# Moving one pair of weight buffers 192 bytes up in SBUF, in a decoder block on one Trainium2 core

## The chip, the core and the metric

The kernel runs on one core of one Trainium2 chip. The metric is the device time of one execution in microseconds (us); the lower, the better. A kernel is timed in several runs, and the median stands for it. One further execution is profiled: its trace gives the start and the duration of each instruction, the waits and the transfers.

## The reference: what is computed

One decoder layer over 512 positions and 1024 channels, in float32. After a normalization, one wide projection feeds a gated short convolution and a sparse attention; both are merged through gates and an output projection and added to x. Then comes the feed-forward part, in which the change lies:

```
h = rmsnorm(x, norm2_g[l])
gu = h @ w_ffn_in[l]
g = causal_dwconv(gu[..., :D_FF], ffn_conv_w[l]) + ffn_conv_b[l]
x = x + (jax.nn.silu(g) * gu[..., D_FF:]) @ w_ffn_out[l]
```

D_FF is 2816, or 22 tiles of 128 channels; `w_ffn_in` has a gate half and an up half.

## The kernel before

**Precision.** All large products run as float32r, with each operand split into a high part and a low part. A product of weights W and activations X is then three matmuls: W high by X high, W high by X low, W low by X high. `dense` (lines 433 to 441) writes them down: for each weight tile first the two with the high weights (lines 437 and 438, alternating), and after all of these the ones with the low weights (line 440). Every matmul has a weight load of its own, of 128 columns (512 bytes in each partition), and TensorE loads the weights of the next matmul while the present one streams.

**The feed-forward input projection** (`ff_strassen`, `ff_forms`, `ff_pair`). Two tiles of 128 output channels are computed together, for the gate half (n = 0) and then for the up half (n = 1): 11 times 2, so 22 pairs. Each pair is one step of Strassen's scheme in Winograd's form: 7 products of quarter size instead of 8. A product has 4 tiles along the contraction and moves 256 positions, so it is 12 matmuls of 128x256, and a pair is 84. The activation forms lie in two long buffers, `xf_h` and `xf_l`, as 4 times 7 blocks of 256 floats. The weight forms of the seven products come from these buffers:

- a22 (one product): `th` (high, two buffers in turn) and `tl` (low), of 2048 bytes in each partition. `dma_split` fills them: ScalarE copies the raw weights into `th` (line 173), writes their negative into `tl` (line 174), and a DMA adds the weights again to `tl` (line 175).
- a11 and a12 (two products): `wh_s` and `wl_s`, from a ring that the down projection uses as well.
- the four sums of quarters: `sh` and `sl`, filled by `split` (lines 167 and 168).

**The down projection** (`down_part`) has matmuls of 128x512 with weights `wh_d` and `wl_d` from the same ring and activations `ah` and `al`; a part is two output tiles of 12 matmuls.

**Order of the work.** The scheduler orders each engine's instructions. In the long steady part of the feed-forward, from about 444 us of the span on, TensorE runs pair after pair as the code has it: the a22 product first (eight matmuls with `th`, four with `tl`), then the other six products (72 matmuls), then one part of the down projection (24 matmuls), then the next pair. Before that, between about 347 and 444 us, products of two pairs and parts of the down projection are interleaved.

**Where the buffers lie.** A partition of SBUF is one range of addresses. The pools `px` and `pw` lie behind one another and are filled in the order of the first request for each name; that is what the two lines of the change set. These are the starts in each partition, in bytes, of the program before, and what is left when they are divided by 128:

| Buffer | Start | mod 128 |
|---|---|---|
| `xf_h`, `xf_l` (moving, pairs) | 37152, 65824 | 32, 32 |
| `th`, two buffers | 94496, 96544 | 32, 32 |
| `gap_w` (never read or written) | 98592 | - |
| `tl`, two buffers | 98784, 100832 | 96, 96 |
| `sh`, first; `sl`, first | 111072; 123360 | 96; 96 |
| ring `wh` (`wh_s`, `wh_d`), first; ring `wl`, first | 204768; 217056 | 96; 96 |
| `ah`, first; `al`, first (moving, down projection) | 138720; 153056 | 96; 96 |

All further buffers of a name, and all slices that a matmul reads of them, lie whole multiples of 512 bytes on, so that the last column holds for each matmul. In words: a matmul of a pair moves data that start at 32 modulo 128; its weights start at 96, other than those of `th`, which start at 32 as the moving data do. In the down projection both start at 96.

Of the kernel before, what the change touches and what calls it, by code (L numbers as in the profile page):

```python
# [11 lines left out]
F32 = mybir.dt.float32  # L12
# [6 lines left out]
P = 128  # L19
# [66 lines left out]
def tile_block(ctx: ExitStack, tc: tile.TileContext, xT, pos, par, par2, w_tok, w_a3, w_gate, w_ao, w_bo, w_o,  # L86
# [13 lines left out]
    def const(shape, name, dt=F32, pool=sb):  # L100
        return pool.tile(shape, dt, name=name, tag=name)
# [798 lines left out]
    xf_h = const([P, 4, 7, TH], "xf_h", F32R, px)  # L900
    xf_l = const([P, 4, 7, TH], "xf_l", F32R, px)
    pw = ctx.enter_context(tc.tile_pool(name="pw", bufs=1, side="left"))
    pw.tile([P, D // 2], F32R, name="th_", tag="th", bufs=2)
    const([P, 48], "gap_w", F32, pw)

    def x_forms(k, v):
        nc.vector.tensor_sub(v[:, T1:T3 + 1], v[:, 1:4:2], v[:, 0:2])
# [282 lines left out]
```

## Time and profile before

| | us |
|---|---|
| Median of 3 runs | 696.2 (695.93 to 697.58) |
| The profiled execution: its own time | 696.92 |
| its span, first to last instruction | 695.1 |
| TensorE busy (matmul) | 689.2 |
| TensorE busy (weight load) | 614.5 |
| VectorE busy | 511.7 |
| ScalarE busy | 436.7 |
| GpSimd busy | 248.7 |

How to read the profile's rows: PE is TensorE's matmuls, PEld its weight loads, DVE VectorE, ACT ScalarE, POOL GpSimd. Names stand for buffers, with their numbers left out: `p<-xf_h,th` is a matmul into a PSUM tile whose name begins with p, with xf_h as moving data and th as weights. A row of the table by stretches of time has the stretch, its length, then for each engine the busy time and in brackets the number of instructions, the granted clock of TensorE as a share (1.00 is full), and the DMA share and GB/s. That number counts the instructions that run at any moment of the stretch: as a matmul of a pair is shown with some 0.28 us and the next starts after about 0.115 us, it holds two or three that began before. Durations of matmuls overlap and their ends are modelled; what a matmul costs in a stream without gaps is the distance from its start to the start of the next, and this text calls that distance a **step**.

### The profile page before, as it was taken

The page shows a single profiled execution, that of the slowest core. Times are in us where ns is not written, and L with a number is a line of the kernel's source. Part 1 is how long each engine was busy: PE and PEld are TensorE (multiplying, and loading weights), DVE is VectorE, ACT ScalarE, POOL GpSimd, SP SyncE. Part 2 cuts the span into 40 slices and gives each one's busy share as a digit, 9 for nine tenths or more (in the row PEclk, how much of TensorE's full clock was granted, in tenths as well). Part 3 has the DMA queues.
Part 4 walks back from the last instruction along what each step waited for, and adds up shares of the span by engine and source line. Part 5 has one row for each costly group of instructions (what it writes and reads, how often), then busy time and mean ns, then how long its engine had stood idle before and what let it go on. Part 6 is the DMA issues. An engine that isn't in the chain of part 4 may idle for free.

```text
span 695.1 us, 11268 instructions
## 1 busy us (share of the span) xinstructions
PE 689.2 (99%) x4111; PEld 614.5 (88%) x4111; DVE 511.7 (74%) x897; ACT 436.7 (63%) x776; POOL 248.7 (36%) x247
## 2 busy tenths in 40 slices
PE   9999999999999999999999999999999999999997
PEld 9999888887878888788889999999999999999986
DVE  6987886766566546475888999898787787877543
ACT  7635654878888866535776857665566655566530
POOL 4041443477788867462112212121122211112110
PEclk9999999999999999999999999999999999999999
DMA  8333686568666654563586977997877979775665
GB/s 268 113 98 122 170 194 145 132 240 237 222 222 228 195 169 124 193 229 118 130 198 160 219 192 167 245 218 180 215 173 180 210 172 227 174 175 112 132 137 152
DMA packets 57623, 124.87 MB, mean 180 GB/s; under 512 B 5344, under 2 KB 21088, under 8 KB 57568
## 3 DMA queue, kind: packets, MB, share of 16 engines
q1 hardware_dynamic: 35648, 79.39, 35.3%
q0 software_dynamic: 14848, 32.51, 27.4%
q10 hardware_dynamic: 7072, 12.26, 5.5%
q8 instruction: 32, 0.52, 0.3%
q14 instruction: 23, 0.19, 0.1%
HBM read 111.55 MB, written 12.58 MB: 179 GB/s over the span
## 4 chain that ended last, share of the span: by engine, by line
PE 95%; ACT 2%; DMA 1%; POOL 1%; DVE 1%; issue 0%; SPq 0%; ACTq 0%; POOLq 0%
PE p L438 10%; PE p L437 10%; PE p L440 10%; PE pdn L438 6%; PE pdn L437 6%; PE pdn L440 6%; PE pg L437 4%; PE pg L438 4%; PE pg L440 3%; PE pa L438 3%; PE pa L437 3%; PE pa L440 3%; PE po L438 2%; PE po L440 2%; PE po L437 2%; PE pj_s L269 2%
## 5 line engine op out<-in xcount | busy, mean ns | idle before, releaser
L437 PE MATMUL p<-xf_h,sh 128*128 128x256 f32 x336 | 80.6, 277 | 0.0
L438 PE MATMUL p<-xf_l,sh 128*128 128x256 f32 x336 | 80.5, 276 | 0.0
L175 POOL DMA_DIRECT2D wl_s<-in_w_ff_dram x22 | 19.6, 891 | 156.1 <-ACT wl_s L174 154.8
L438 PE MATMUL pdn<-al,wh_d 128*128 128x512 f32 (+1 forms) x176 | 68.5, 389 | 0.0
L437 PE MATMUL pdn<-ah,wh_d 128*128 128x512 f32 (+1 forms) x176 | 68.3, 389 | 0.0
L438 PEld LDWEIGHTS p<-xf_l,sh 128*128 128x128 f32 x336 | 63.1, 188 | 0.0
L437 PEld LDWEIGHTS p<-xf_h,sh 128*128 128x128 f32 x336 | 63.1, 188 | 0.0
L167 ACT ACTIVATE sh<-s 128x1024 fp32r<-128x1024 f32 x44 | 46.3, 1055 | 25.3 <-PE p L438 22.4
L168 DVE TENSOR_TENSOR sl<-s,sh 128x1024 fp32r<-128x1024 f32 x44 | 53.5, 1218 | 8.7 <-ACT sh L167 8.6
L173 ACT ACTIVATE wh_s<-wr_s 128x1024 fp32r<-128x1024 f32 x22 | 23.3, 1060 | 56.9 <-PE pdn L438 54.3
L750 POOL TENSOR_TENSOR tn_e<-tn_e,ph 128x512 fp32r<-128x512 f32 x40 | 51.2, 1294 | 16.2 <-ACT ph L749 16.0
L440 PE MATMUL p<-xf_h,sl 128*128 128x256 f32 x336 | 52.2, 277 | 0.0
L175 POOL DMA_DIRECT2D wl_d<-in_w_dn_dram x22 | 26.7, 1212 | 71.3 <-ACT wl_d L174 71.3
L437 PE MATMUL pg<-xg_h,wh_g 128*128 128x512 f32 x128 | 50.1, 392 | 0.0
L438 PE MATMUL pg<-xg_l,wh_g 128*128 128x512 f32 x128 | 50.1, 391 | 0.0
L440 PE MATMUL pdn<-ah,wl_d 128*128 128x512 f32 (+1 forms) x176 | 47.5, 388 | 0.0
L440 PEld LDWEIGHTS p<-xf_h,sl 128*128 128x128 f32 x336 | 44.7, 188 | 0.2
L1109 DVE TENSOR_TENSOR x<-x,pdn 128x512 f32<-128x512 f32 x47 | 32.0, 682 | 15.9 <-PE pdn L440 15.3
L150 POOL TENSOR_TENSOR wl_g<-wr_g,wh_g 128x1024 fp32r<-128x1024 f32 x16 | 38.5, 2405 | 10.4 <-ACT wh_g L148 9.7
L438 PE MATMUL p<-xf_l,wh_s 128*128 128x256 f32 x168 | 40.6, 277 | 0.0
L437 PE MATMUL p<-xf_h,wh_s 128*128 128x256 f32 x168 | 40.5, 277 | 0.0
L175 POOL DMA_DIRECT2D tl<-in_w_ff_dram x22 | 19.7, 894 | 57.3 <-ACT tl L174 49.7
(367 smaller groups left out, 2117.5 us busy)
## 6 DMA issues: line engine op xcount, KB each, us to landing
wr_s<-in_w_ff_dram SPq DMA_DIRECT2D x44, 512.0 KB, 5.0
wl_s<-in_w_ff_dram POOLq DMA_DIRECT2D x22, 512.0 KB, 7.8
wr_d<-in_w_dn_dram ACTq DMA_DIRECT2D x22, 512.0 KB, 8.3
wl_d<-in_w_dn_dram POOLq DMA_DIRECT2D x22, 512.0 KB, 9.0
wr_g<-in_w_gate_dram SPq DMA_DIRECT2D x16, 512.0 KB, 4.0
wr_a<-in_w_a_dram SPq DMA_DIRECT2D x12, 512.0 KB, 3.7
tl<-in_w_ff_dram POOLq DMA_DIRECT2D x22, 256.0 KB, 7.6
td_e<-e SPq DMA_DIRECT2D x16, 256.0 KB, 4.4
```

The lines of the kernel that those rows point to most:

```text
L150: e.tensor_sub(lo[:, 0:n], raw[:, 0:n], hi[:, 0:n].bitcast(F32))
L167: hi = nc.scalar.activation(h, v, AF.Copy)
L168: nc.vector.tensor_sub(l, v, h.bitcast(F32))
L173: nc.scalar.activation(h, raw, AF.Copy)
L175: nc.gpsimd.dma_start(l if dst is None else dst, src, accum_op=ALU.add)
L269: nc.tensor.matmul(acc, xg_h[:, k, ts_], wh, start=k == 0, stop=False)
L437: ops.append(nc.tensor.matmul(acc, wh, xh, start=first and i == 0, stop=False))
L438: ops.append(nc.tensor.matmul(acc, wh, xl, start=False, stop=False))
L440: nc.tensor.matmul(acc, wl, xh, start=False, stop=last and i == len(units) - 1)
L750: nc.gpsimd.tensor_sub(pl, pt, ph.bitcast(F32))
L1109: nc.vector.tensor_add(xj, xj, acc)
```

## The change

In the pool `pw`, the request for the 192 bytes of `gap_w` is moved from behind the request for `th` to ahead of it. The two buffers of `th` so start at 94688 and 96736, which is 96 modulo 128, where they started at 32; the gap lies at 94496. `tl` and all other buffers stay where they were, and the pool has the same size. On each engine the same instructions stand in the same order as before.

```diff
     pw = ctx.enter_context(tc.tile_pool(name="pw", bufs=1, side="left"))
+    const([P, 48], "gap_w", F32, pw)
     pw.tile([P, D // 2], F32R, name="th_", tag="th", bufs=2)
-    const([P, 48], "gap_w", F32, pw)
```

## The prediction

> **What bounds the kernel now.** I read the page first, for the engine that is never idle, then the same by stretches for the part of the span that the change touches.
>
> ```profile
> span 695.1 us, 11268 instructions
> PE 689.2 (99%) x4111; PEld 614.5 (88%) x4111; DVE 511.7 (74%) x897; ACT 436.7 (63%) x776; POOL 248.7 (36%) x247
> 360.00:690.00 330.00, 330.00 (x2368) 309.09 (x2367) 261.40 (x364) 194.17 (x256) 63.10 (x65) 1.00 0.78 181
> ```
>
> TensorE is busy for all 330.00 us of the feed-forward part, at a granted clock of 1.00, and nobody else comes near (VectorE 261.40). So here the time is the number of matmuls times their step, and a nanosecond that is put on a step or taken from it is seen at the end. No transfer, wait or order of instructions changes: what is left is what an address does to the step of a matmul. About 0.3% (2.1 us) is what a measurement of this kernel can tell from no change.
>
> Next I looked for a trace of the address in the groups by line and shape, mean ns behind the busy time:
>
> ```profile
> L437 PE MATMUL p<-xf_h,sh 128*128 128x256 f32 x336 | 80.6, 277 | 0.0
> L438 PE MATMUL p<-xf_l,th 128*128 128x256 f32 x84 | 21.1, 282 | 0.0
> L437 PE MATMUL p<-xf_h,th 128*128 128x256 f32 x84 | 21.0, 281 | 0.0
> L440 PE MATMUL p<-xf_h,tl 128*128 128x256 f32 x84 | 13.1, 277 | 0.0
> ```
>
> Same shape, same moving data, and `th` alone is 4 to 5 ns longer; `th` is also the one weight buffer that starts at 32 modulo 128 as the moving data do (the table of starts). `tl`, written from the same raw weights and read with the same block of `xf_h`, has 277. That looks like a small cost that the change takes away. But a mean can hide two values, so the third view is TensorE alone by stretches, cut at the starts of products (columns: stretch, length, PE busy with its count, clock, DMA share, GB/s). The counts hold two matmuls that began before the stretch (in two rows three).
>
> ```profile
> 358.83:360.84 2.01, 2.01 (x19) 1.00 1.05 220
> 374.08:404.50 30.42, 30.42 (x269) 1.00 0.91 219
> 379.30:380.25 0.95, 0.95 (x10) 1.00 1.02 403
> 406.34:411.76 5.42, 5.42 (x48) 1.00 0.96 232
> 411.76:412.71 0.95, 0.95 (x11) 1.00 1.04 377
> 412.71:417.69 4.98, 4.98 (x46) 1.00 0.34 105
> 424.09:428.45 4.36, 4.36 (x39) 1.00 0.39 161
> 443.90:444.85 0.95, 0.95 (x10) 1.00 1.12 276
> 444.85:453.46 8.61, 8.61 (x78) 1.00 0.88 197
> 453.46:458.93 5.47, 5.47 (x27) 1.00 0.95 215
> 655.22:663.83 8.61, 8.61 (x78) 1.00 0.69 150
> 443.90:669.30 225.40, 225.40 (x1622) 1.00 0.79 180
> ```
>
> The rows at 379.30, 411.76 and 443.90 are runs of eight matmuls with `th`: 0.95 / 8 = 118.8 ns a step. All other rows but 453.46 and the last hold matmuls of pairs with `wh_s`, `wl_s`, `sh`, `sl` or `tl` (that at 374.08 has three `th` runs within it), all with weights at 96 and moving data at 32. And these go at two paces: 358.83 with 2.01 / 17 = 118.2 ns, 406.34 with 5.42 / 46 = 117.8 and 424.09 with 4.36 / 37 = 117.8; but 412.71 with 4.98 / 44 = 113.2, 444.85 with 8.61 / 76 = 113.3 and 655.22 with the same. The clock is 1.00 in all of them, and the DMA share goes with neither (0.39 and 0.96 at the long pace, 0.34 and 0.91 at the short one). I call them the long pace (117.8) and the short pace (113.3).
>
> What switches between them is seen in the timeline (start, duration), at the end of one down part and the start of another pair:
>
> ```profile
> 405.89 0.39 PE L437 MATMUL pdn<-ah,wh_d 128*128 128x512 f32 x1
> 406.11 0.39 PE L438 MATMUL pdn<-al,wh_d 128*128 128x512 f32 x1
> 406.34 0.40 PE L437 MATMUL p<-xf_h,wh_s 128*128 128x256 f32 x2
> ...
> 423.18 1.07 PE L440 MATMUL pdn<-ah,wl_d 128*128 128x512 f32 x4
> 424.09 0.52 PE L440 MATMUL p<-xf_h,tl 128*128 128x256 f32 x3
> ```
>
> Where matmuls of a pair directly follow the 512-wide ones of the down or output projection, and their own weights start at 96, they take the long pace and keep it: the stretches 406.34 and 424.09 begin so, and 358.83 likewise behind the output projection. In the first of them 46 matmuls with `wh_s`, `wl_s`, `sh` and `sl` change nothing about it. Then comes the run of eight with `th` at 411.76, and behind it stands 113.2 ns. In the steady part a down part always comes ahead of `th`, and the pace behind `th` is short each time, from 444.85 to 655.22. So `th` does two things: it pays 118.8 ns a step itself, and it leaves the stream at the short pace for the 76 matmuls that follow, until the next 512-wide part loses it.
>
> **The change part by part.** ScalarE's writes and the DMA are not touched: `th` alone moves, the DMA of line 175 goes to `tl`, and the copy into `th` is off the path, since TensorE waits for nothing in 330 us. What TensorE reads is the whole change.
>
> *The `th` run itself, in the steady part.* With weights at 96 behind a down part it is what `wh_s` at 406.34 and `tl` at 424.09 are: eight steps of 117.8, or 0.942 us where 0.95 stands now, a gain of 0.008 us a pair. If the stream stayed at the short pace it would be 0.906, a gain of 0.044: that is the other end of this term.
>
> *The 76 matmuls behind it.* No matmul with weights at 32 comes any more, so nothing in the rows above brings the stream back from the long pace. 76 x (117.8 - 113.3) = 76 x 4.54 = 0.345 us a pair. The other end is zero, if the pace comes back by itself at once; I take the full value because the rows of matmuls at 96 behind a 512-wide one stay long for as far as they reach (46 and 37 matmuls), with each kind of weight buffer in them. The down part's own 5.47 us stay: it is entered from the short pace now and from the long one then, and I price that at nothing (its 24 matmuls start and end at 96 and 96 in both).
>
> *How many pairs.* One period is 0.95 + 8.61 + 5.47 = 15.03 us, and 225.40 / 15.03 is 15 pairs. So 15 x (0.345 - 0.008) = +5.06 us.
>
> *The interleaved stretch ahead of it.* From 412.71 to 417.69 the 44 matmuls at 113.2 go long as well: 44 x 4.6 = +0.20. From 374.08 to 404.50 no 512-wide matmul intervenes, and I expect the short pace to stay as it is; the three `th` runs in it then go at the short pace too: 3 x (0.95 - 8 x 0.1134) = -0.13 us. The remaining `th` runs, at 411.76 and 420, lie at the long pace already, so nothing.
>
> *Sum.* 5.06 + 0.20 - 0.13 = +5.1 us. Against the profiled execution's own 696.92 that gives 702.0; it lies 0.7 above the median of 696.2, for which I forecast 701.3. No cover is needed: TensorE is the bound before and after, and the others only gain time.
>
> The rows speak against a rule of the Trainium skill here. The page "SBUF — State Buffer", section "Who interferes with whom", gives TensorE two independent read ports, for moving data and for weights, and says "PE and ACT never wait on anyone"; the page "TensorE: Matmul & The Clock Gate", section "Step-by-step: what each phase is for", adds that loading the next weights takes no read bandwidth from the running matmul. By these the sum would be zero. The trace does not agree: 118.8 ns against 113.3 for matmuls that differ in the start of their weights.
>
> **The rivals.**
>
> *The small gain (faster side).* If the long pace came from something else in the neighbourhood of those stretches, the 168 matmuls with `th` would fall to 113.3 and the rest would stay: 168 x (118.8 - 113.3) = 0.92 us less, 695.3. For it: it is the plain reading of 282 against 277, and 15 of the pairs have no long step outside their `th` run today. Against it: the stretch 406.34, which has no `th` in it or near ahead of it and is long from its first matmul to its last. The point from which it decides: the `th` run can win 0.044 us a pair, and a long step costs 0.0045, so with ten long steps left in a pair of 84 the gain is gone.
>
> *The pace returns within the pair.* The longest unbroken row at the long pace behind a 512-wide part is 46 matmuls, and a pair has 84. If it came back half-way, 5.1 would be about 2.5, and the time 698.7. Nothing in the trace shows such a return; but nothing shows 84 without one either.
>
> *The short pace is lost earlier.* Its first appearance, at 374.08, isn't owed to a run of `th`:
>
> ```profile
> 373.15 0.28 PE L437 MATMUL p<-xf_h,wh_s 128*128 128x256 f32 x1
> ...
> 373.74 0.40 PE L419 MATMUL pr_n<-dg_n,ones 128*128 128x512 f32 x1
> 373.97 0.28 PE L438 MATMUL p<-xf_l,wh_s 128*128 128x256 f32 x1
> 374.08 0.62 PE L440 MATMUL p<-xf_h,wl_s 128*128 128x256 f32 x4
> ```
>
> There a 512-wide matmul with the weights `ones` (which do not start at 96) brings it. If it came out otherwise with `th` moved, the stretch 374.08 to 404.50 would be long too: (30.42 - 2.86) / 113.4 ns are 243 steps, 243 x 4.4 = 1.1 us, and the 0.13 would not come back: 702.5.
>
> *The address doesn't matter at all*, and `th` is dearer because it comes first in its pair: 696.2. Against it: at 379.30 a `th` run stands in the middle of the short pace, with no 512-wide matmul ahead of it, and has 118.8 all the same.
>
> **How the numbers follow.** The forecast, +5.1, has 0.62; the loss from 374 on 0.12; a return within the pair 0.10; the small gain 0.13; no effect 0.03. Slower by over 0.3%, or by over 2.1 us, are the first two and nearly all of the third: 0.83. Within 0.3% are the small gain, no effect and what is left: 0.16. Faster by over 0.3%, 0.01: the whole price of `th` is below 1 us. The range has the first three cases, 0.84 of the chance, from 698.7 to 702.5 and 0.7 above that for the spread of the runs (the profiled execution lies so far from the median): 698.7 to 703.2.
>
> **What would show it right or wrong.** In the changed kernel's trace, by the same stretches of the steady part: a period of 15.37 us where 15.03 stands, the eight `th` matmuls at 117.8 ns a step and the 76 behind them at 117.8 (8.95 us). The means of the groups: `sh` and `wh_s` go up from 277 towards 280, `th` down from 282 towards 280, all alike. The stretch before 404.50 stays at 113.4. It is wrong if the 76 stand at 113.3 (then the small gain is the case, and `th` does not carry the pace), or if the matmuls behind a down part start at 118 and fall to 113 in the middle of a pair.

## The result and the profile after

The changed kernel takes 702.84 us (median of 4 runs, 702.24 to 703.52) beside 696.54 for the kernel before on the same chip (4 runs, 695.93 to 697.58). The ratio is 1.0089, with a 95% interval of 1.0075 to 1.0103: 6.3 us slower. The profiled execution took 703.28, with a span of 701.5 us against 695.1: 6.4 us that can be looked for in the trace.

The page of the kernel after: TensorE is busy 6.2 us longer (695.4 against 689.2) with the same 4111 matmuls, and stays at 99%.

```profile
span 701.5 us, 11268 instructions
PE 695.4 (99%) x4111; PEld 620.3 (88%) x4111; DVE 512.7 (73%) x897; ACT 436.7 (62%) x776; POOL 247.4 (35%) x247
```

Two groups of it, by line and shape (busy time, mean ns of one):

```profile
L437 PE MATMUL p<-xf_h,sh 128*128 128x256 f32 x336 | 82.9, 279 | 0.0
L438 PE MATMUL p<-xf_l,th 128*128 128x256 f32 x84 | 20.9, 280 | 0.0
```

`th` has come down from 282 to 280, and `sh`, which wasn't touched, has gone up from 277 to 279. The second outweighs the first, since there are many more of the others. By these means alone the loss would still look small; the steps show its size. TensorE by stretches, cut at the same instructions as before (stretch, length, busy time with its count, clock, DMA share, GB/s):

```profile
373.83:405.28 31.45, 31.45 (x269) 1.00 0.84 210
413.49:418.43 4.94, 4.94 (x44) 1.00 0.51 187
445.09:446.03 0.94, 0.94 (x9) 1.00 1.15 259
446.03:454.98 8.95, 8.95 (x78) 1.00 0.96 236
454.98:460.46 5.48, 5.48 (x26) 1.00 0.82 172
661.26:670.21 8.95, 8.95 (x78) 1.00 0.68 153
445.09:675.69 230.60, 230.60 (x1622) 1.00 0.78 177
```

The 76 matmuls behind `th` take 8.95 us in the first steady pair and in the last, where 8.61 stood: 117.8 ns a step for 113.3, at a clock of 1.00 both times. The steady part is 230.60 us for 225.40, so 5.20 of the 6.4 us lie there. The stretch before the down projection begins, 373.83 to 405.28, has 31.45 us for 30.42: another 1.03. The last 0.4 lie around 418: the 42 steps from 413.49 to 418.43 are at 117.6 ns (4.94 us; before, the same 42 had 4.76, from 412.71 to 417.47), which is 0.18; and the four steps behind them (two of the pair, two of the down part) have 0.90 us where 0.69 stood, which is 0.21. With the 0.25 us by which this execution was ahead at 373.83 (374.08 before), the steady part begins 1.19 later (445.09 for 443.90), and 1.19 + 5.20 = 6.39 is the whole difference.

The 0.21 has a look of its own. TensorE and ScalarE at that place in the kernel after (start, duration; in brackets the idle time and what ended it):

```profile
418.55 0.28 PE L438 MATMUL p<-xf_l,sh 128*128 128x256 f32 x1
418.77 0.72 PE L437 MATMUL pdn<-ah,wh_d 128*128 128x512 f32 x2
419.33 0.28 PE L437 MATMUL p<-xf_h,sh 128*128 128x256 f32 x1
```

```profile
416.10 0.63 ACT L173 ACTIVATE th<-wr_s 128x512 fp32r<-128x512 f32 x1 [3.82 <-DMA wr_s<-in_w_ff_dram]
418.11 1.14 ACT L167 ACTIVATE ah<-up 128x512 fp32r<-128x512 f32 x2
```

The matmuls that read `ah` start while ScalarE is still writing its two halves (418.11 to 419.25); ScalarE is late because the copy into `th` ahead of it waited for raw weights until 416.10. This is a small stall, at a place that comes back below. The raw weights don't land there at the same time in each execution: the copy into `th` at this place starts at 414.06 in the kernel before, and between 413.42 (experiment 4) and 416.10 (here) in the traces whose order of work is the same.

### The profile page after: what moved, and what is told of

It is laid out like the page before. It is cut to its first block, busy times and chain, and to the rows that moved or that the text cites. A ratio compares the mean times of both kernels' runs of the same rounds, so it can differ in the third digit from the quotient of the medians.

```text
span 701.5 us, 11268 instructions
## 1 busy us (share of the span) xinstructions
PE 695.4 (99%) x4111; PEld 620.3 (88%) x4111; DVE 512.7 (73%) x897; ACT 436.7 (62%) x776; POOL 247.4 (35%) x247
## 4 chain that ended last, share of the span: by engine, by line
PE 89%; DMA 3%; ACT 3%; POOL 2%; DVE 1%; issue 1%; SPq 0%; ACTq 0%; POOLq 0%; DVEq 0%
PE p L437 10%; PE p L440 10%; PE p L438 10%; PE pdn L437 6%; PE pdn L438 6%; PE pdn L440 6%; PE pg L438 3%; PE pg L437 3%; PE pg L440 3%; PE pa L438 3%; PE pa L437 3%; PE pa L440 3%; PE po L438 2%; PE po L437 2%; PE po L440 2%; PE pj_s L269 2%
## 5 line engine op out<-in xcount | busy, mean ns | idle before, releaser
L437 PE MATMUL p<-xf_h,sh 128*128 128x256 f32 x336 | 82.9, 279 | 0.0
L438 PE MATMUL p<-xf_l,sh 128*128 128x256 f32 x336 | 82.8, 279 | 0.0
```

Of the source, the lines that this page charges most:

```text
L437: ops.append(nc.tensor.matmul(acc, wh, xh, start=first and i == 0, stop=False))
L438: ops.append(nc.tensor.matmul(acc, wh, xl, start=False, stop=False))
```

## The experiments

The theory was that of the prediction: the run of eight `th` matmuls, whose weights start where the moving data start, brings the short pace, and everything else in a pair only keeps the pace that it finds. Against it stood two rivals: that the place of `th` in memory as such (its address, its neighbours) sets the pace, or the place of the a22 product in the order, first behind the down part. What "start where the moving data start" means was open too: the table speaks of 128 bytes, and the period could be another. So `th` was first moved by other distances.

All kernels compute the whole result. Their edits are told against the kernel before, unless another is named. Below, **distance** is the start of the weights less the start of the moving data, modulo 256 (why 256 is the outcome of the second and of the eleventh experiment). From the table of starts, the kernel before has 0 for `th`, 192 for all other weights of a pair, and 0 in the down part; the kernel after has 192 for `th`.

**1. `th` higher by 64 bytes instead of 192** (distance 64).

```diff
+    const([P, 16], "gap_v", F32, pw)
     pw.tile([P, D // 2], F32R, name="th_", tag="th", bufs=2)
-    const([P, 48], "gap_w", F32, pw)
+    const([P, 32], "gap_w", F32, pw)
```

> The two th buffers lie 64 bytes higher than before (192 in the change), so at 96 modulo 128 as in the change. Theory (what counts is whether weights and moving data start alike modulo 128; a run that starts alike leaves the short pace): the same as the change, eight th matmuls and the 76 behind them at 117.8 ns in each pair of the steady part, and a time 5 to 6.5 us above the kernel before. Rival (it is this one place of the buffers, 192 bytes up, or a larger period than 128): the pairs stand at 113.3 as before, and the time is within 1 us of it.

Measured: 702.2 us against 697.05, ratio 1.0071 (1.0054 to 1.0089). TensorE by stretches, around the first `th` run behind the matmuls with `ones`, then a steady pair:

```profile
378.31:379.72 1.41, 1.41 (x14) 1.00 0.98 240
379.72:380.63 0.91, 0.91 (x11) 1.00 1.02 394
380.63:387.54 6.91, 6.91 (x63) 1.00 0.49 154
521.93:530.88 8.95, 8.95 (x78) 1.00 0.79 178
```

The steady pairs are long, as in the kernel after. But at 379.72 the `th` run, entered at the long pace from other matmuls of a pair (1.41 / 12 = 117.5 ns), goes at 113.8 (0.91 / 8) and leaves the short pace (6.91 / 61 = 113.3). So the same buffer can bring the short pace in one place and not in another: what counts is not the distance alone, but also what the run is entered from.

**2. `th` higher by 128 bytes** (32 modulo 128, as before; distance 128).

```diff
+    const([P, 32], "gap_v", F32, pw)
     pw.tile([P, D // 2], F32R, name="th_", tag="th", bufs=2)
-    const([P, 48], "gap_w", F32, pw)
+    const([P, 16], "gap_w", F32, pw)
```

> The two th buffers lie 128 bytes higher than before, so at 32 modulo 128 again. Theory: as before to within 0.3%, th runs of 0.95 us and 76 matmuls at 113.3 ns behind them. Rival (any move away from the old place, or from its distance to tl, costs): 5 to 6 us above before.

Measured: 702.34, ratio 1.0072 (1.0057 to 1.0087): not as before, but as after. TensorE by stretches, at the same two places:

```profile
374.58:379.00 4.42, 4.42 (x41) 1.00 0.99 198
379.95:388.54 8.59, 8.59 (x75) 1.00 0.68 178
522.49:531.44 8.95, 8.95 (x78) 1.00 0.86 183
```

The period of 128 bytes, on which the table of starts and the prediction's working rest, is not it. At 379.00 the run even takes the short pace away: 4.42 / 39 = 113.3 ns ahead of it, 8.59 / 73 = 117.7 behind it.

**3. All addresses as before, the a22 product last in its pair.**

```diff
-        product(b45[:, lo], "a22", T4)
...
         product(b45[:, hi], 1, T1)
+        product(b45[:, lo], "a22", T4)
```

> All buffers lie as before; the a22 product comes last of the seven in a pair where it came first. Theory: the six products between the down part and the th run go at the long pace, 72 matmuls x 4.5 ns = 0.33 us a pair in the steady part, so 4.5 to 6 us above before, with tl behind th at 113.3. Rival (what counts is where the buffers lie, and th is only dearer itself): within 1 us of before, all matmuls but those of th at 113.3.

Measured: 701.9, ratio 1.0064 (1.0049 to 1.0079). TensorE by stretches through one steady pair: 72 matmuls of the other products, the `th` run, four `tl`:

```profile
520.58:529.07 8.49, 8.49 (x74) 1.00 0.67 162
529.07:530.02 0.95, 0.95 (x11) 1.00 1.09 252
530.02:530.47 0.45, 0.45 (x6) 1.00 0.74 137
```

The 72 behind the down part are long (117.9 ns), and the four `tl` behind the `th` run short (113 ns): 15 x 72 x 4.54 ns = 4.9 us, and 4.85 were measured. No address is moved here, so the same loss comes without any buffer at another place; and the pace changes at the `th` run itself, whether that comes first or last.

**4. `th` of the gate half as before, `th` of the up half 64 bytes higher.**

```diff
-    pw.tile([P, D // 2], F32R, name="th_", tag="th", bufs=2)
-    const([P, 48], "gap_w", F32, pw)
+    pw.tile([P, D // 2], F32R, name="th0_", tag="th0", bufs=1)
+    const([P, 16], "gap_v", F32, pw)
+    pw.tile([P, D // 2], F32R, name="th1_", tag="th1", bufs=1)
+    const([P, 32], "gap_w", F32, pw)
...
-        h = pw.tile([P, HALF_D], F32R, name=f"th{nm}", tag="th", bufs=2)
+        h = pw.tile([P, HALF_D], F32R, name=f"th{nm}", tag=f"th{n}", bufs=1)
```

> One of the two th buffers (that of the gate half) lies as before, the other (the up half) 64 bytes higher. Theory: in the steady part pairs of the gate half have 76 matmuls at 113.3 and pairs of the up half at 117.8, in turn; 8 of 15 pairs then are 0.34 us longer, and the time is 2.5 to 3.5 us above before. Rival (the pace is a matter of the whole execution, set early and kept): all pairs at one pace, 0 or 5 to 6.5 us above before.

Measured: 699.58, ratio 1.0036 (1.0024 to 1.0048). Two steady pairs in turn, each the `th` run and the 76 behind it:

```profile
520.09:521.04 0.95, 0.95 (x9) 1.00 0.57 196
521.04:529.65 8.61, 8.61 (x78) 1.00 0.86 190
535.12:536.07 0.95, 0.95 (x9) 1.00 0.13 47
536.07:545.02 8.95, 8.95 (x78) 1.00 0.68 139
```

Short and long alternate with the buffer, within one execution: 8 long pairs x 0.345 = 2.8 us, and 2.5 were measured. The `th` run itself is 0.95 in both. So the loss is not in `th`, but behind it, and each pair is decided anew.

**5. `xf_h`, `xf_l`, `th`, `tl`, `sh` and `sl` all higher by 64 bytes, the rings where they were** (distance 0 for `th` as before, 192 for `tl`, `sh`, `sl`, but 128 for `wh_s` and `wl_s`).

```diff
-    const([P, 80], "gap_x", F32, px)
+    const([P, 96], "gap_x", F32, px)
```

> The gap ahead of xf_h is 64 bytes longer, so that xf_h, xf_l, th, tl, sh and sl all lie 64 bytes higher than before and the rings stay: moving data, th, wh_s and wl_s start at 96, tl, sh and sl at 32. Theory (only the likeness of weights and moving data counts): th and the 24 matmuls with wh_s and wl_s have steps near 119 to 120, the 52 with tl, sh and sl 113.3; 24 x 6 ns = 0.15 us more a pair than before, 2 to 3.5 us in all. Rival (weights that start at 32 are dear by themselves): the 52 with tl, sh and sl are dear at 118 or more, th and wh_s are not, 3 to 5 us above before.

Measured: 703.14 against 697.06, ratio 1.0086 (1.0071 to 1.0101), 6.1 us more and so above both stretches of the expectation. Behind the `th` run of a steady pair: `tl`, the 24 with `wh_s` and `wl_s`, the 48 with `sh` and `sl`:

```profile
522.42:522.88 0.46, 0.46 (x7) 1.00 0.33 133
522.88:525.71 2.83, 2.83 (x26) 1.00 0.72 191
525.71:531.37 5.66, 5.66 (x51) 1.00 0.92 170
```

The `th` run, at another address but at distance 0, still brings the short pace in the steady pairs: the four `tl` have 0.457 us, the first three steps of them 113 to 114 ns (0.471 in the kernel after, where all four are long). Behind the three `th` runs between 378 and 399 it doesn't come (0.48). Then 24 matmuls at distance 128 go at 118 and take the pace away, and the 48 behind them, at 192 as ever, keep the long one. It is the distance of weights to moving data that works, and a product at distance 128 undoes it, as in experiment 2.

**6 and 7. `ah` and `al` lower by 64 bytes**, in the kernel after (6) and in the kernel before (7): the 512-wide matmuls of the down part, at distance 0 in both kernels, go to 64.

```diff
     a_tiles(0)
+    const([P, 16], "gap_a", F32, pf)
```

> The changed kernel with the moving data of the down projection (ah and al) 64 bytes lower, so that these start at 32 and their weights at 96: no matmul of the steady part then starts alike. Theory: nothing takes the short pace away and nothing brings it back, so all pairs of the steady part keep the one pace that the early part leaves them: either 113.3 throughout (then 1 to 2 us below before) or 117.8 throughout (then as the change). Rival (a 512-wide part takes the pace away whatever its starts): 117.8, as the change.

> The kernel before with ah and al 64 bytes lower. Theory: the th run still brings the short pace, and the down part, no longer alike, is shorter: its first eight matmuls lose the 26 ns a part that they have now, and each step may lose 1 ns; 0.5 to 1.2 us below before. Rival (the down part's entry costs the same whatever its starts): within 0.3 us of before.

Measured: in the kernel after 705.87, ratio to before 1.0124 (1.0109 to 1.0139); in the kernel before 699.26, ratio 1.0027 (1.0015 to 1.0039), where I had expected a gain. A down part and what follows, first in 6, then in 7:

```profile
532.37:537.97 5.60, 5.60 (x27) 1.00 0.89 230
538.91:547.86 8.95, 8.95 (x79) 1.00 0.67 131
```

```profile
528.50:534.08 5.58, 5.58 (x26) 1.00 0.97 248
535.04:543.65 8.61, 8.61 (x78) 1.00 0.64 125
```

The down part's own step goes from 228 to 233 ns (5.60 / 24), 0.12 us a part dearer in both; the paces behind it in the steady part stay as they were. So the distance has a price for the 512-wide matmuls too, and there 0 is the cheaper one.

**8. The kernel after, with `tl` moved as well, to distance 0**: four matmuls at distance 0 behind the eight at 192. The edit moves more than that: its three gaps add up to 320 bytes where there were 192, so that all that lies behind `tl` in the pool starts 128 bytes higher, `sh` and `sl` too. These go from distance 192 to 64.

```diff
-    pw.tile([P, D // 2], F32R, name="th_", tag="th", bufs=2)
     const([P, 48], "gap_w", F32, pw)
+    pw.tile([P, D // 2], F32R, name="th_", tag="th", bufs=2)
+    const([P, 16], "gap_v", F32, pw)
+    pw.tile([P, D // 2], F32R, name="tl_", tag="tl", bufs=2)
+    const([P, 16], "gap_u", F32, pw)
```

> th lies as in the change (96), and tl instead lies at 32 modulo 128, with the moving data. Theory: a run of four matmuls with tl that starts alike comes ahead of 72 others; if four are enough they leave the short pace, and the time is 0.3 to 0.8 us above before at most (eight th matmuls at the long pace); if it takes more than four, 5 to 6.5 us above. Rival (it is th's own place): as the change, whatever tl does.

Measured: 699.53, ratio 1.0033 (1.002 to 1.0047). Behind the `th` run of a steady pair: `tl`, the 24 with `wh_s` and `wl_s`, the 48 with `sh` and `sl`:

```profile
521.34:521.82 0.48, 0.48 (x6) 1.00 0.41 115
521.82:524.64 2.82, 2.82 (x26) 1.00 0.83 224
524.64:530.10 5.46, 5.46 (x50) 1.00 0.92 162
```

The four `tl` at distance 0 don't bring the short pace to what follows them: the 24 behind have 2.82 / 24 = 117.5 ns. The 48 with `sh` and `sl` have 5.46 / 48 = 113.8, the first three of them still 116 to 123 ns and the rest 113 to 114; so the pace changes where the matmuls at distance 64 begin, as it did at the `th` run in the early part of experiment 1, also at 64. The 76 are then 0.15 us dearer than before (8.76), which is 2.2 us in 15 pairs. It is not `sh` at 64 alone: from 405.69 on, behind a down part and with no `tl` ahead, 46 matmuls, 28 of them with `sh` and `sl`, stay long (5.42 us). What the `tl` run adds isn't separated here, since two things were moved at once.

**9 and 10. `ah` and `al` lower by 192 bytes**, in the kernel before (9) and in the kernel after (10): the down part goes to distance 192.

```diff
     a_tiles(0)
+    const([P, 48], "gap_a", F32, pf)
```

> The kernel before with ah and al 192 bytes lower, so that the weights of the down projection start 192 bytes above the moving data modulo 256 or 512, as those of sh, sl, tl and wh_s do in a pair. Theory (what counts is how the start of the weights stands to that of the moving data, modulo 256 or more; a distance of 192 keeps the pace that it finds): the down part no longer takes the short pace away and has no dear entry, 24 steps of 226 to 227 in 5.43 us where 5.46 stands, the th run is entered at the short pace and has 0.96 us as in the early part; 0.2 to 0.8 us below before. Rival (512-wide parts always end at the long pace): down parts as before or longer, time within 0.5 us of before or above.

> The changed kernel with ah and al 192 bytes lower. Theory: nothing in the steady part changes the pace, so it stays as the early part leaves it: in the changed kernel that was the long one, so 117.8 in all pairs, and 5 to 6 us above before; if it is short it is so throughout, 1 us below before. Rival (the down part itself sets the pace): all pairs at 117.8 whatever the early part leaves.

Measured: 9, in the kernel before, 701.23 against 697.0, ratio 1.0059 (1.0043 to 1.0076), where I had expected a small gain. 10, in the kernel after, 696.97, ratio to before 0.9998 (0.9989 to 1.0008), where 5 to 6 us above or 1 us below was expected: the loss of the change is gone, with `th` where the change puts it. In 9 the steady pairs come in threes, two long and one short; the 76 of a short one, a down part, and `th` and the 76 of the long one that follows:

```profile
521.47:530.08 8.61, 8.61 (x79) 1.00 0.83 173
530.08:535.57 5.49, 5.49 (x26) 1.00 0.96 247
535.57:536.53 0.96, 0.96 (x9) 1.00 0.18 73
536.53:545.48 8.95, 8.95 (x78) 1.00 0.70 147
```

In 10 the short pace comes from the down part, and a steady pair with its down part keeps it:

```profile
432.17:433.42 1.25, 1.25 (x13) 1.00 0.95 213
519.78:520.69 0.91, 0.91 (x10) 1.00 0.83 306
520.69:529.30 8.61, 8.61 (x78) 1.00 0.90 197
529.30:534.79 5.49, 5.49 (x26) 1.00 0.92 235
```

The pair's first matmuls behind a down part at 432.17 are short already (1.25 / 11 = 113.6 ns), and `th` at 192 doesn't touch the pace: 0.91 / 8 = 113.8. So the 512-wide matmuls at distance 0 are the other half of the cause. In the steady part they leave the stream at the long pace each time (experiment 3 and the kernel after); a run at distance 0 behind them mends it; in the kernel after, nothing does. And in 9 the same `th` at distance 0 leaves two pairs of three long, so that "a `th` run brings the short pace" holds behind the down part of the kernel before, and is no rule by itself.

**11. `th` higher by 256 bytes** (distance 0 again).

```diff
+    const([P, 64], "gap_v", F32, pw)
     pw.tile([P, D // 2], F32R, name="th_", tag="th", bufs=2)
-    const([P, 48], "gap_w", F32, pw)
+    const([P, 112], "gap_w", F32, pw)
```

> The two th buffers lie 256 bytes higher than before (and all behind them in the pool 512 bytes higher, the same modulo 512). If the period is 256, all is as before: th runs of 0.95 us, 113.3 ns behind them, within 0.3% of before. If it is 512 or more, th stands otherwise to the moving data than before, and the pairs may go long: up to 6 us above.

Measured: 696.77, ratio 0.9998 (0.9986 to 1.0011). The 76 behind a steady `th` run:

```profile
534.96:543.57 8.61, 8.61 (x78) 1.00 0.69 143
```

All as before. 64, 128 and 192 bytes are each long behind the down part, 256 is short again: of the distances tried, the period is 256 bytes.

**12. Experiment 1 (`th` 64 higher) together with `ah` and `al` 192 lower**, an attempt at a kernel that beats both: short steps in the steady part from the one, cheap `th` runs in the early part from the other.

> th 64 bytes higher (as in e1_up64) and ah and al 192 bytes lower (as in e10_after_ah192). Theory, from the steps of those two runs: the th run costs nothing at the short pace (0.907 us) and turns the long pace of the early part short at about 380 us, and the down part of 5.49 us leaves the short pace behind it; a steady period of 15.01 us where before has 15.03, the early pairs at 113.3, and a time 0.2 to 1.2 us below before (about 0.1%). Rival (the early part comes out long, or a th run 64 bytes up goes long behind the down part as it did in e1_up64): within 0.3 us of before in the one case, 5 us above in the other.

Measured: 697.79 against 696.84, ratio 1.0007 (0.9997 to 1.0017): no gain. A steady pair with its down part:

```profile
519.02:519.94 0.92, 0.92 (x9) 1.00 0.77 252
519.94:528.55 8.61, 8.61 (x78) 1.00 0.85 191
528.55:534.05 5.50, 5.50 (x27) 1.00 0.98 246
```

0.92 + 8.61 + 5.50 = 15.03, which is the period before: what `th` wins (0.03), the down part at distance 192 pays. And ahead of the steady part TensorE waits, in the timeline of the same kernel:

```profile
417.71 0.74 PE L437 MATMUL pdn<-ah,wh_d 128*128 128x512 f32 x2 [1.64 <-ACT ah L167]
```

It is the place of the small stall in the kernel after. TensorE came here at 416.07, 1.6 us earlier than in the kernel before (417.69); most of that lead it had when the first `th` run of the part began (359.29 for 360.84), ahead of anything that the edit touches. The wait takes all of it back, and 417.71 is where the kernel before is. ScalarE, ahead of `ah`, had waited for raw weights until 415.04, a microsecond later than it begins the same copy in the kernel before (414.06). Why they came later no run shows; a lead ahead of this place is lost when they do.

## Why the prediction was right, and where it failed

The forecast was +5.1 us; measured were +6.3 between the medians and +6.4 in the profiled execution. The main mechanism came out as forecast, and one step ahead of it did not. That combination is the third rival, to which the prediction gave 0.12; its 702.5 lies next to the median of 702.84.

**The main term.** "76 x (117.8 - 113.3) = 76 x 4.54 = 0.345 us a pair", 15 times, less 0.008 a pair for `th`: +5.06, measured +5.20. The 76 have 8.95 for 8.61 as forecast; the `th` run has 0.94 where 0.942 was forecast, and the down part 5.48 for 5.47, so that the period is 15.37 as forecast (230.60 / 15). Experiments 3 and 4 show the step behind it: with no address changed, the matmuls ahead of the `th` run are long and those behind it short; and pair by pair the pace goes with the start of `th`.

**The step that failed.** "From 374.08 to 404.50 no 512-wide matmul intervenes, and I expect the short pace to stay as it is": it didn't come about in the first place. The forecast here was -0.13; measured was +1.03, and the third rival had named this with 1.1 us. These 1.16 us are most of what the forecast lacks. The timeline of the kernel after at the two matmuls with `ones`:

```profile
372.69 0.39 PE L419 MATMUL pr_n<-dg_n,ones 128*128 128x512 f32 x1
372.92 0.28 PE L437 MATMUL p<-xf_h,wh_s 128*128 128x256 f32 x1
...
373.38 0.28 PE L437 MATMUL p<-xf_h,wh_s 128*128 128x256 f32 x1
373.49 0.39 PE L419 MATMUL pr_n<-dg_n,ones 128*128 128x512 f32 x1
373.72 0.28 PE L438 MATMUL p<-xf_l,wh_s 128*128 128x256 f32 x1
```

The first matmul with `ones` brings the short pace (from 372.92 to 373.49 five steps of 114 ns), and the second takes it away again: behind it come 31.45 us at the long pace. In the kernel before it is the second that leaves the short pace. That `ones` brings the short pace was taken for a property of `ones`. But it goes with what ran long before: behind `ones` the pace is long in the kernel after and in experiments 6 and 10, all with `th` at 192; it is short in 4, 7, 9 and 11, with the `th` of the gate half at 0, and in 2, with `th` at 128. (The others don't compare: in 1, 8 and 12 `ones` is entered from the short pace, in 3 the order is another, in 5 `wh_s` lies at another distance.) The last `th` of that place starts at 370.22 in the kernel after and at 370.44 before; from there to the first `ones`, 2.5 us on, both kernels run the same instructions with the same addresses at the long pace, and then come out of `ones` differently. So more is carried along than which of the two paces it is. What that is wasn't taken apart and stays open.

**Sizes around 418.** Forecast +0.20; measured +0.18 from the pace, and 0.21 more from the stall for `ah`, which no term had. That ScalarE's late copy of `ah` is the cause of this 0.21 is argued from the two timelines; in experiments 8, 9, 10 and 12 the profile shows the same wait outright (1.03, 0.28, 0.51 and 1.64 us). And it need not belong to the change: in experiment 6, which has the paces of the kernel after up to here, the copy into `th` starts at 413.62 in place of 416.10, and the two matmuls of the down part have 0.46 us, without a stall.

**The picture behind it.** "`th` is also the one weight buffer that starts at 32 modulo 128 as the moving data do" was true and not to the point: 128 bytes higher the buffer is as bad as in the change (experiment 2), and 256 bytes higher as good as before (experiment 11). The forecast came out all the same, because 192 bytes is no multiple of either; that was luck. Moved by 128 bytes, the same working would have forecast no loss, as the expectation of experiment 2 did.

**Small gain or no effect.** Both fell with the 8.95: `th` did win its 0.01 us a pair, and the 76 lost 0.34. The rule of the Trainium skill's page "SBUF — State Buffer", section "Who interferes with whom", that TensorE reads weights and moving data through two independent ports, was taken to mean no change; the measurement disagrees with that by 6.3 us, and in experiment 4 by 0.34 us from one pair to the next with the same instructions at the same clock.

**What stays open.** That the distance of weights to moving data sets the loss is shown: it comes and goes with `th` (experiments 4 and 11) and with the moving data of the down part (10), and with no address moved it stands ahead of the `th` run when that comes last (3). Why there are two paces, why a pace is kept, and why the same distance acts otherwise from another entry, no run shows; the traces hold starts and waits, and nothing of what happens inside a matmul.

## What to carry to other kernels

Where TensorE never waits, read the distance from start to start of its matmuls in stretches, rather than mean durations: a group mean moved by 2 ns where the stream had lost 4.5 ns a step for whole products. Before a buffer is moved because its own matmuls look dear, see what the matmuls behind it do, and try the other side as well: the moving data of the matmuls ahead (experiment 10) undid the whole loss of 0.9%. And look for the next wait downstream before counting an early gain, since one stall for a late buffer (1.64 us) can take it back.

## What the runs showed of the hardware

- Matmuls of 128x256 in a stream without gaps go at 113.3 or 117.8 ns a step, at a granted clock of 1.00 with the same operands, and keep the pace for whole products. Where it changed in the stretches shown, matmuls at another distance or 512-wide ones stood at that place.
- The distance of weights to moving data works with a period of 256 bytes among those tried: behind a down part at distance 0, `th` at 0 and at 256 leaves the short pace, at 64, 128 and 192 the long one.
- The 512-wide matmuls of the down part have 228 ns a step at distance 0 (5.47 / 24; 5.49 in experiment 5), 229 at 192 (5.49 / 24) and 233 at 64 (5.60 / 24).
- In experiment 9 the pace repeats over three pairs (long, long, short) though each pair has the same instructions and the same distances: something is carried over from one pair to the next.
